# Storing an attention gate's z raw and taking its silu later, in a fused attention and convolution block

## The chip, the cores and the metric

The kernel runs on one core of a Trainium2 chip. A core has TensorE (PE in the profile, with its weight loads as PEld), VectorE (DVE), ScalarE (ACT), GpSimd (POOL) and SyncE (SP); DMAs are issued from the queues of SP, ACT and POOL. The metric is the device time of one execution in microseconds. Before the change the median of three runs is 644.86 us (642.94 to 645.86).

## The reference

One layer of a diffusion transformer on 1024 latent tokens (a grid of 16 rows and 64 columns) of width 1024, with 256 context tokens, all in fp32. The steps that matter here:

```python
h = rmsnorm(x, norm_g) * (1 + scale[:, None]) + shift[:, None]
q, k, v, za, u, bg, cg, zc = jnp.split(h @ w_in, SPLIT_POINTS, axis=-1)   # 8 parts of 512 columns
# q, k: RMS norm per head, rotary; kc, vc: the same columns of the context
attn = neighbourhood_attention(q, k, heads(v), kc, vc, rpb) * jax.nn.silu(za)
conv = bg * centred_short_conv(cg * u, conv_w, conv_b) * jax.nn.silu(zc)
x_new = x + gate[:, None] * (jnp.concatenate([attn, conv], axis=-1) @ w_out)
```

The attention has 8 heads of width 64. A query sees a window of 8 x 16 latent tokens with a learned bias, and all 256 context tokens, in one softmax.

## The kernel before

Every product in fp32 is made of three matmuls on high and low parts (`mm3`, L74 to L76): ACT copies the high part, DVE subtracts to get the low one. The program has three stages.

*Projections.* `h` is made and kept in SBUF with tokens along the free axis. A loop over 4 pairs of heads and 8 token tiles (32 steps, `NT`, and three more to drain) makes q, k and v for a pair, normalises and rotates them and writes them to DRAM (`q_d`, `k_d`, `v_d`). The exponent of that norm is on POOL; ACT does squares, copies and scaling.

*Attention.* It runs as 36 quarters (`quarter(n)`, L1063): quarter n computes scores for the pieces of head n // 4, turns those of quarter n - 2 into probabilities, and multiplies those of quarter n - 3 with v. In a quarter PE first transposes the running maxima `mx` (into `pmx`), DVE takes the row maxima `rm`, PE spreads them back and ACT copies them out as `mg`; DVE subtracts `mg` from the scores `sc` and `sb`, ACT takes exps twice (once rounded, `phc` and `phl`, once full), POOL and DVE subtract to get the low parts `plc` and `pll`. In the same quarter PE makes the new scores `pss` (latent) and `pc` (context, L970; ACT copies them to `sc`), and DVE adds the bias and updates `mx` for the quarter after next. When a head half is done ACT copies its output `po` to `ob` and issues two stores from its own queue, the row sums (`rs_d`) and the output (`o_d`, `finish`, L1035).

*Filler.* The remaining projections, of z for the four pairs (`attn_group(f)`, L484) and of u, c, z and b for three convolution groups (`conv_group`, L384), are units of two halves with four ticks each (`unit(col)`, L338); a tick is six matmuls `pu`. `TICKS` (L33) says how many ticks a quarter takes, so that a unit ends with a quarter: the attention gates' units end with the projections and with quarters 2, 5 and 8, the z units of convolution groups 1 and 2 with quarters 16 and 26, that of group 3 after the quarters. A tick asks for the next unit's weights (`uraw`), ACT and DVE split them (`uh`, `ul`). What a finished unit leaves for ACT and DVE is queued with `chore` and emitted by `do_acts` at the end of a quarter and `do_dves` in the next.

*Gating.* When a pair's last output is stored (quarters 11, 19, 27 and 35), a generator `gated(p)` (L1263) starts, one step a quarter: it loads the row sums, takes reciprocals on DVE, stores them, loads silu(z), the output and the reciprocals of each half, multiplies twice and stores to `y_d`. The last pair is gated in the output stage (`put_y`, L1330).

*Output.* `y` is loaded and split for the eight groups in the order `FORDER`, with `w_out`, and multiplied; six tiles are made group by group, so each group is needed only some 4 us after the one ahead of it.

On PE, ACT, DVE and POOL the program order of the attention is kept as written (the class `ordered`); SP's DMAs may be moved by the scheduler. A queue runs in order. Each DMA has one of eight semaphores, given in turn, and waits until the DMA eight places ahead has landed. ACT loads another function table when the next function is not in the loaded one: silu and exp are in different tables, squares, copies and scaling go with both.

Of the kernel before, what the change touches and what calls it, by code (L numbers as in the profile page):

```python
# [19 lines left out]
P = 128  # L20
# [19 lines left out]
def body(tc, es, x, ctxt, w_ada, b_ada, w_in, q_g, k_g, rpbr, w_out, vecs, cst, out):  # L40
# [49 lines left out]
    def many(name, n, shape):  # L90
        return [dr.tile(shape, F32, name=f"{name}{i}")[:] for i in range(n)]
# [6 lines left out]
    g_d = dr.tile([1, D], F32, name="g_d")  # L98
    rope_d = dr.tile([P, 2048], F32, name="rope_d")
    rs_d = many("rs_d", NPAIR, [2, 2, 512])  # L100
    zs_d = many("zs_d", NPAIR, [P, T])


    q_d = many("q_d", NH, [2, HD, 4, 2, 256])
# [196 lines left out]
    def chore(on_act=None, on_dve=None, queue=soon, frees=None):  # L301
        queue.append([on_act, on_dve, frees])
        if act not in strict:
            do_acts()
            do_dves()

    def do_acts():
        for c in soon + (slow if not any(c[1] and c[1].__name__ == "product" for c in soon) else []):
            if c[0]:
                c[0]()  # L310
                c[0] = None
# [72 lines left out]
    def conv_group(i, done=None):  # L384
# [89 lines left out]
        for part in (gains, gates) if done else (gates, gains):  # L474
            yield from part()

    def silus(z):
        out = []
        for half, ps in z:
            out.append(cvp.tile([P, 512], F32, name="zs", tag="ub", bufs=2))  # L480
            act.activation(out[half], ps, AF.Silu)
        return out

    def attn_group(f):  # L484

        z = []
        for got in unit(z_col(f)):
            if got:
                z.append(got)
            else:  # L490
                yield

        def on_act():
            for half, zs in enumerate(silus(z)):
                sp.dma_start(zs_d[f][:, half * 512:(half + 1) * 512], zs)
        chore(on_act)

    def recip(p, pl):

# [563 lines left out]
    def quarter(n):  # L1063

        live = lambda m: 0 <= m < 4 * NH
        ticks = TICKS[n]
        e, o = n - 2, n - 3  # L1070
        if live(e):
            hd, g = heads[e // 4], e % 4
            pm = psm.tile([P, 512], F32, name="pmx", tag="C", bufs=2)
            for i in range(2):
                pe.transpose(pm[:, i * P:(i + 1) * P], mx[:, (2 * g + i) * P:(2 * g + i + 1) * P], ident)
            rm = ap.tile([P, 2], F32, name="rm", tag="rm", bufs=8)
            dve.tensor_reduce(rm, pm[:, :256].rearrange("p (i k) -> p i k", i=2), AX.X, ALU.max)
        if live(o):
            heads[o // 4].ctx_out(o % 4)
        do_dves(3)  # L1080
        if gating and next(gating[0], "end"):
            gating.clear()
        if live(e):
            for i in range(2):
                pe.transpose(pm[:, 256 + i * P:256 + (i + 1) * P], rm[:, i:i + 1].broadcast_to([P, P]), ident)
            act.copy(mg[:, g * 256:(g + 1) * 256], pm[:, 256:512])
        now = pair_of(n)
        for i, hd_, j in now:
            hd_.scores(j, sbank[:, i])
        if live(n):  # L1090
            heads[n // 4].ctx_scores(n % 4)
        if live(e):
            hd.ctx_exp(g)
        if e in sbs or e in exps:
            pair, sb = pair_of(e), sbs.pop(e)
            w = both(sb, e, pair)
            dve.tensor_tensor(w, w, maxima_of(e, pair), ALU.subtract)
            exps[e] = [ap.tile([P, 2, 384], F32R, name=m, tag=m, bufs=2) for m in ("phl", "pll")]
            ph, pl = (both(v, e, pair) for v in exps[e])
            act.activation(ph, w, AF.Exp)  # L1100
            act.activation(w, w, AF.Exp)
        for _ in range(1):
            next(fill, None)
        done = []
        if o >= 0:
            pho, plo = exps.pop(o)
            for i, hd_, j in pair_of(o):
                hd_.lat_out(j, pho[:, i], plo[:, i])
                if j in (4, 7):
                    done.append((hd_, j // 7))  # L1110
                    if j == 7 and hd_.s:
                        ready.append(hd_.p)
        if now:
            sb = sbs[n] = sb_new()
            g_ = n % 4
            if g_:
                bt = now[0][1].bt
                bias = bt[:, 1:2].broadcast_to([P, 2, 384]) if g_ == 2 else bt[:, 0:2] if g_ == 1 else bt[:, 1:3]
                dve.tensor_tensor(sb, sbank[:, :, :384], bias, ALU.add)
            else:  # L1120
                for i, hd_, j in now:
                    cols = slice(P, 384) if j == 0 else slice(0, 256)
                    dve.tensor_tensor(sb[:, i, :256], sbank[:, i, :256], hd_.bt[:, 1, cols], ALU.add)
            if live(n):
                heads[n // 4].ctx_max(n % 4)
            for i, hd_, j in now:
                hd_.lat_max(j, sb[:, i])
        if e in sbs or e in exps:
            dve.tensor_tensor(pl, w, ph.bitcast(F32), ALU.subtract)
        for _ in range(ticks - 1):  # L1130
            next(fill, None)
        for hd_, bank_ in done:
            hd_.finish(bank_)
        do_acts()
# [32 lines left out]
    for n in range(NT + 3):  # L1167
# [11 lines left out]
            gate.load(n - 1)  # L1179
        if 9 <= n < 25 and n % 2:  # L1180
            next(tables)
        if n == NT - 6:
            heads[0].masks()
            heads[0].load_k()
# [78 lines left out]
    def gated(f):  # L1263

        ri = ap.tile([P, 16], F32, name="ri", tag="ri", bufs=4)
        sp.dma_start(ri, rs_d[f].rearrange("h b (x c) -> (h b x) c", c=16))
        yield
        dve.reciprocal(ri, ri)
        sp.dma_start(ri_d[f].rearrange("h (x c) -> (h x) c", c=16), ri)
        yield  # L1270
        for half in range(2):
            cols = slice(half * 512, (half + 1) * 512)
            zs, tb, rb = (ap.tile([P, 512], F32, name=n, tag=n, bufs=1) for n in ("zs", "tb", "rb"))
            sp.dma_start(zs, zs_d[f][:, cols])
            sp.dma_start(tb, o_d[f][:, cols])
            load_sums(f, half, rb, sp)
            yield
            dve.tensor_tensor(zs, zs, rb, ALU.mult)
            yield
            dve.tensor_tensor(tb, tb, zs, ALU.mult)  # L1280
            sp.dma_start(y_d[f][:, cols], tb)

    with sbuf("att") as ap, psum("psb") as psb:
        sbank = psb.tile([P, 2, 512], F32, name="pss")
        strict[:] = every
        mx = ap.tile([P, T], F32, name="mx")
        sb_new = lambda: ap.tile([P, 2, 384], F32, name="sb", tag="sb", bufs=3)
        mg = ap.tile([P, T], F32, name="mg")
        heads[0].load_v()
        for n in range(4 * NH + 4):  # L1290
            h, g = divmod(n, 4)
            if 0 < h < NH and g == 0:
                heads[h].load_v()
            if h + 1 < NH and g:
                nx = heads[h + 1]
                for load in ((nx.masks, nx.load_q), (nx.load_k,), ())[g - 1]:
                    load()
            quarter(n)
            if ready:
                p = ready.pop()  # L1300
                if p < NPAIR - 1:
                    gating[:] = [gated(p)]
                else:
                    recip(p, ap)
        for _ in fill:
            do_dves()
            do_acts()
        while soon or slow:
            do_dves()
            do_acts()  # L1310
        strict[:] = []
# [18 lines left out]
    def put_y(yp, f):  # L1330

        yh = yp.tile([P, T], F32R, name=f"yh{f}")
        yl = yp.tile([P, T], F32R, name=f"yl{f}")
        for half in range(2):
            cols = slice(half * 512, (half + 1) * 512)
            tb = op.tile([P, 512], F32, name="tb", tag="zt", bufs=4)
            if f == NPAIR - 1:
                zs = op.tile([P, 512], F32, name="zs", tag="zt", bufs=4)
                rb = op.tile([P, 512], F32, name="rb", tag="rb", bufs=2)
                act.dma_start(zs, zs_d[f][:, cols])  # L1340
                act.dma_start(tb, o_d[f][:, cols])
                load_sums(f, half, rb, pool)
                dve.tensor_tensor(zs, zs, rb, ALU.mult)
                dve.tensor_tensor(tb, tb, zs, ALU.mult)
            else:
                act.dma_start(tb, y_d[f][:, cols])
            tv = blocked(tb[:]) if f < NPAIR else by_row(tb[:])
            act.copy(natural(yh[:], half), tv)
            dve.tensor_tensor(natural(yl[:], half), tv, natural(yh[:].bitcast(F32), half), ALU.subtract)
        y[f] = yh, yl  # L1350
# [88 lines left out]
```

## Time and profile before

| | |
|---|---|
| median of three runs | 644.86 us |
| the profiled execution | 644.16 us, span 642.4 us |
| PE busy | 628.7 us (98%) |
| DVE busy | 432.3 us (67%) |
| ACT busy | 322.1 us (50%) |
| POOL busy | 131.6 us (20%) |
| ACT_TABLE_LOAD | 13, 1283 ns each |
| ACT silu of 128x512 | 16, about 600 ns each |

A row of a timeline gives the start in us, the duration, the engine, the line of the kernel, the operation, output<-input by the program's names, the shape, the count of merged instructions and, in brackets, the idle time of the engine just before and what ended it. Most lines read L55, since a recording helper issues the instruction; the names of the tiles tell them apart. `SPq` and `ACTq` are DMA issues. A row of windows gives a stretch, its length and, for each engine, its busy time and its number of instructions. The projections end and quarter 0 begins at about 271.7 us (the first `pss`); the output stage begins at about 550 us.

### The profile page before, as it was taken

What the parts mean: (1) busy time and instruction counts of PE and PEld (TensorE: products, weight loads), DVE (VectorE), ACT (ScalarE), POOL (GpSimd) and SP (SyncE); (2) the same over time, 40 slices, a digit from 0 to 9 for tenths busy, and PEclk for the clock granted to TensorE, in tenths of its full rate; (3) what the DMA queues carried; (4) which work ended last, traced back from release to release, by engine and by line L of the source; (5) the groups of instructions that cost most, each with busy time, mean ns of one, the idle gap of its engine ahead of it and who ended that gap; (6) DMA issues with size and microseconds to landing.
All of it is one profiled execution on the core that took longest, in us unless ns stands there. A gap on an engine that the chain in (4) does not pass through costs nothing.

```text
span 642.4 us, 10301 instructions
## 1 busy us (share of the span) xinstructions
PE 628.7 (98%) x3479; PEld 537.2 (84%) x3480; DVE 432.3 (67%) x819; ACT 322.1 (50%) x692; POOL 131.6 (20%) x138
## 2 busy tenths in 40 slices
PE   8999999999999999999999999999999999999997
PEld 3477898999899999877787888888888888788885
DVE  1677838865766855458787899988998864475111
ACT  3676815524624445347776658565675644352000
POOL 1205005123122222001111121121111111004421
PEclk9999999999999999999999999999999999999999
DMA  8973465868785898799866758785852223875621
GB/s 317 382 255 103 123 221 173 251 210 223 227 276 147 262 273 234 198 233 218 200 161 174 202 146 225 188 212 148 232 144 90 68 89 123 281 239 201 215 100 49
DMA packets 118864, 125.46 MB, mean 195 GB/s; under 512 B 32817, under 2 KB 89353, under 8 KB 117532
## 3 DMA queue, kind: packets, MB, share of 16 engines
q1 hardware_dynamic: 112348, 113.23, 61.0%
q10 hardware_dynamic: 6208, 11.05, 5.6%
q0 software_dynamic: 256, 0.54, 0.3%
q8 instruction: 27, 0.44, 0.3%
q14 instruction: 25, 0.20, 0.1%
HBM read 88.01 MB, written 38.53 MB: 197 GB/s over the span
## 4 chain that ended last, share of the span: by engine, by line
PE 66%; DMA 13%; DVE 9%; SPq 6%; ACT 3%; issue 2%; POOL 1%; ACTq 0%; DVEq 0%; POOLq 0%
PE pu L55 18%; PE pacc L55 18%; DMA k_s<-k_d 5%; PE po L55 5%; PE pout L75 4%; PE pout L76 4%; PE pout L74 4%; SPq L55 3%; PE cacc L55 3%; PE acc L55 2%; PE tr L55 2%; DVE mx L55 2%; DVE sb L55 2%; PE pss L55 2%; PE pmx L55 2%
## 5 line engine op out<-in xcount | busy, mean ns | idle before, releaser
L55 PE MATMUL pu<-h,uh 128*128 128x512 f32 x544 | 169.0, 392 | 0.0
L55 PE MATMUL pacc<-wh,h 128*128 128x384 f32 x512 | 135.3, 338 | 0.0
L55 PEld LDWEIGHTS pu<-h,uh 128*128 128x128 f32 x544 | 98.2, 188 | 17.0
L55 PE MATMUL pu<-h,ul 128*128 128x512 f32 x272 | 106.3, 391 | 0.0
L55 PEld LDWEIGHTS pacc<-wh,h 128*128 128x128 f32 x512 | 92.9, 188 | 0.2 <-ACT qn L55 0.2
L55 POOL TENSOR_TENSOR plc<-sc,phc 128x512 fp32r<-128x512 f32 x32 | 42.6, 1330 | 221.3 <-ACT sc L55 112.3
L55 PE MATMUL pacc<-wl,h 128*128 128x384 f32 x256 | 85.6, 335 | 0.0
L55 POOL TENSOR_TENSOR ss<-ss,few 128x4 f32<-128x4 f32 (+1 forms) x40 | 41.9, 1050 | 127.6 <-DVE ss L55 127.3
L55 PEld LDWEIGHTS pu<-h,ul 128*128 128x128 f32 x272 | 51.1, 188 | 11.2
L55 DVE TENSOR_TENSOR mx<-mx,sb 128x384 f32<-128x384 f32 (+1 forms) x64 | 55.6, 877 | 2.0
L75 PE MATMUL pout<-wol,yh 128*128 128x512 f32 x128 | 49.9, 390 | 0.2 <-DVE wol L1327 0.2
L76 PE MATMUL pout<-woh,yl 128*128 128x512 f32 x128 | 49.6, 389 | 0.0
L74 PE MATMUL pout<-woh,yh 128*128 128x512 f32 x128 | 48.3, 389 | 0.0
L55 PEld LDWEIGHTS pacc<-wl,h 128*128 128x128 f32 x256 | 48.1, 188 | 0.1
L55 DVE TENSOR_REDUCE ss<-sq 128x4 f32<-128x260 f32 (+1 forms) x40 | 15.8, 394 | 46.3 <-ACT sq L55 46.2
L55 ACT COPY mg<-pmx 128x256 f32<-128x256 f32 x32 | 12.0, 374 | 60.1 <-PE pmx L55 48.2
L55 ACT ACTIVATE sq<-pacc 128x256 f32<-128x256 f32 x32 | 12.3, 385 | 53.3 <-PE pacc L55 52.4
L1371 DVE TENSOR_TENSOR ot<-pout,gate 128x512 f32<-128x512 f32 x16 | 10.9, 689 | 37.6 <-PE pout L76 35.3
L55 DVE TENSOR_TENSOR pll<-sb,phl 128x768 fp32r<-128x768 f32 (+2 forms) x33 | 29.3, 889 | 7.5 <-ACT sb L55 7.5
L1372 POOL TENSOR_TENSOR ot<-ot,xr 128x512 f32<-128x512 f32 x15 | 20.1, 1345 | 67.5 <-DVE ot L1371 65.9
L55 ACT ACTIVATE qn<-pacc,ss 128x64 f32<-128x64 f32 x128 | 30.0, 329 | 6.7 <-POOL ss L55 3.2
L55 DVE TENSOR_TENSOR sc<-sc,mg 128x512 f32<-128x512 f32 x32 | 21.9, 683 | 16.4 <-ACT mg L55 16.4
(151 smaller groups left out, 1276.3 us busy)
## 6 DMA issues: line engine op xcount, KB each, us to landing
uraw<-in_w_in SPq DMA_DIRECT2D x34, 256.0 KB
q_d<-qs SPq DMA_DIRECT2D x64, 128.0 KB
k_s<-k_d SPq DMA_DIRECT2D x16, 512.0 KB
q_s<-q_d SPq DMA_DIRECT2D x32, 256.0 KB
wr<-in_w_in SPq DMA_DIRECT2D x40, 192.0 KB
slab<-in_w_ada SPq DMA_DIRECT2D x6, 1024.0 KB
t_d<-btw SPq DMA_DIRECT2D x8, 576.0 KB
bt<-t_d SPq DMA_DIRECT2D x8, 576.0 KB
```

The lines of the kernel that those rows point to most:

```text
L55: i = emit(*a, **kw)
L74: i = pe.matmul(ps, ah, bh, start=first, stop=False)
L75: pe.matmul(ps, ah, bl, start=False, stop=False)
L76: pe.matmul(ps, al, bh, start=False, stop=last)
L1371: dve.tensor_tensor(ot, ps, gate[:, cols], ALU.mult)
L1372: (dve if (nh, t) == (1, NB - 1) else pool).tensor_tensor(ot, ot, xr, ALU.add)
```

## The change

The attention gates' units no longer take the silu when they finish. Each half of z is copied by ACT from PSUM as soon as that half is finished and stored raw in `z_d`. When a pair is gated, both halves of z are loaded at once, at the generator's first step, and put in a list `held`; the next call of `silus`, that of a convolution group's z unit, takes their silu on ACT behind its own, and gating goes on after that. For pair 2 a call of `silus` is queued at once, because no convolution group's unit ends within the quarters after it. For the last pair the silu is taken in the output stage. `gating` becomes a list of generators, worked off one after the other, and what is left of it after the quarters is finished there. An exp of one column in step 29 of the projections has the table of exp loaded there. In quarter 0 the first tick of filler stands ahead of the context scores.

```diff
@@ -98,7 +98,7 @@
     g_d = dr.tile([1, D], F32, name="g_d")
     rope_d = dr.tile([P, 2048], F32, name="rope_d")
     rs_d = many("rs_d", NPAIR, [2, 2, 512])
-    zs_d = many("zs_d", NPAIR, [P, T])
+    z_d = many("z_d", NPAIR, [P, T])
 
 
     q_d = many("q_d", NH, [2, HD, 4, 2, 256])
@@ -474,26 +474,30 @@
         for part in (gains, gates) if done else (gates, gains):
             yield from part()
 
+    held = []
+
     def silus(z):
         out = []
         for half, ps in z:
             out.append(cvp.tile([P, 512], F32, name="zs", tag="ub", bufs=2))
             act.activation(out[half], ps, AF.Silu)
+        while held:
+            for v in held.pop():
+                act.activation(v, v, AF.Silu)
         return out
 
     def attn_group(f):
 
-        z = []
+        def keep(half, ps):
+            z = cvp.tile([P, 512], F32, name="z", tag="ub", bufs=2)
+            act.copy(z, ps)
+            sp.dma_start(z_d[f][:, half * 512:(half + 1) * 512], z)
+
         for got in unit(z_col(f)):
             if got:
-                z.append(got)
+                chore(lambda got=got: keep(*got))
             else:
                 yield
-
-        def on_act():
-            for half, zs in enumerate(silus(z)):
-                sp.dma_start(zs_d[f][:, half * 512:(half + 1) * 512], zs)
-        chore(on_act)
 
     def recip(p, pl):
 
@@ -1079,7 +1083,7 @@
             heads[o // 4].ctx_out(o % 4)
         do_dves(3)
         if gating and next(gating[0], "end"):
-            gating.clear()
+            gating.pop(0)
         if live(e):
             for i in range(2):
                 pe.transpose(pm[:, 256 + i * P:256 + (i + 1) * P], rm[:, i:i + 1].broadcast_to([P, P]), ident)
@@ -1087,6 +1091,9 @@
         now = pair_of(n)
         for i, hd_, j in now:
             hd_.scores(j, sbank[:, i])
+        if n == 0:
+            next(fill)
+            ticks -= 1
         if live(n):
             heads[n // 4].ctx_scores(n % 4)
         if live(e):
@@ -1099,7 +1106,7 @@
             ph, pl = (both(v, e, pair) for v in exps[e])
             act.activation(ph, w, AF.Exp)
             act.activation(w, w, AF.Exp)
-        for _ in range(1):
+        for _ in range(n > 0):
             next(fill, None)
         done = []
         if o >= 0:
@@ -1127,7 +1134,7 @@
                 hd_.lat_max(j, sb[:, i])
         if e in sbs or e in exps:
             dve.tensor_tensor(pl, w, ph.bitcast(F32), ALU.subtract)
-        for _ in range(ticks - 1):
+        for _ in range(ticks - (n > 0)):
             next(fill, None)
         for hd_, bank_ in done:
             hd_.finish(bank_)
@@ -1179,6 +1186,8 @@
             gate.load(n - 1)
         if 9 <= n < 25 and n % 2:
             next(tables)
+        if n == NT - 3:
+            act.activation(few[:, 5:6], ones, AF.Exp)
         if n == NT - 6:
             heads[0].masks()
             heads[0].load_k()
@@ -1264,21 +1273,29 @@
 
         ri = ap.tile([P, 16], F32, name="ri", tag="ri", bufs=4)
         sp.dma_start(ri, rs_d[f].rearrange("h b (x c) -> (h b x) c", c=16))
+        cols = [slice(half * 512, (half + 1) * 512) for half in range(2)]
+        zs = [ap.tile([P, 512], F32, name="zs", tag="zs", bufs=2) for _ in cols]
+        for v, c in zip(zs, cols):
+            sp.dma_start(v, z_d[f][:, c])
         yield
         dve.reciprocal(ri, ri)
         sp.dma_start(ri_d[f].rearrange("h (x c) -> (h x) c", c=16), ri)
+        held.append(zs)
+        if f == NPAIR - 2:
+            chore(lambda: silus(()))
         yield
-        for half in range(2):
-            cols = slice(half * 512, (half + 1) * 512)
-            zs, tb, rb = (ap.tile([P, 512], F32, name=n, tag=n, bufs=1) for n in ("zs", "tb", "rb"))
-            sp.dma_start(zs, zs_d[f][:, cols])
-            sp.dma_start(tb, o_d[f][:, cols])
+        while held:
+            yield
+        for v, c in zip(zs, cols):
+            tb, rb = (ap.tile([P, 512], F32, name=n, tag=n, bufs=1) for n in ("tb", "rb"))
+            half = cols.index(c)
+            sp.dma_start(tb, o_d[f][:, c])
             load_sums(f, half, rb, sp)
             yield
-            dve.tensor_tensor(zs, zs, rb, ALU.mult)
+            dve.tensor_tensor(v, v, rb, ALU.mult)
+            dve.tensor_tensor(tb, tb, v, ALU.mult)
+            sp.dma_start(y_d[f][:, c], tb)
             yield
-            dve.tensor_tensor(tb, tb, zs, ALU.mult)
-            sp.dma_start(y_d[f][:, cols], tb)
 
     with sbuf("att") as ap, psum("psb") as psb:
         sbank = psb.tile([P, 2, 512], F32, name="pss")
@@ -1299,9 +1316,13 @@
             if ready:
                 p = ready.pop()
                 if p < NPAIR - 1:
-                    gating[:] = [gated(p)]
+                    gating.append(gated(p))
                 else:
                     recip(p, ap)
+        for step in gating:
+            for _ in step:
+                do_acts()
+                do_dves()
         for _ in fill:
             do_dves()
             do_acts()
@@ -1337,9 +1358,10 @@
             if f == NPAIR - 1:
                 zs = op.tile([P, 512], F32, name="zs", tag="zt", bufs=4)
                 rb = op.tile([P, 512], F32, name="rb", tag="rb", bufs=2)
-                act.dma_start(zs, zs_d[f][:, cols])
+                act.dma_start(zs, z_d[f][:, cols])
                 act.dma_start(tb, o_d[f][:, cols])
                 load_sums(f, half, rb, pool)
+                act.activation(zs, zs, AF.Silu)
                 dve.tensor_tensor(zs, zs, rb, ALU.mult)
                 dve.tensor_tensor(tb, tb, zs, ALU.mult)
             else:
```

## The prediction

> **What bounds the kernel now.** I read the busy time of each engine first, then the busy time by stage, then by quarter of the attention, and last the timelines of ACT, DVE and PE at the quarters that are too long.
>
> ```profile
> span 642.4 us, 10301 instructions
> ## 1 busy us (share of the span) xinstructions
> PE 628.7 (98%) x3479; PEld 537.2 (84%) x3480; DVE 432.3 (67%) x819; ACT 322.1 (50%) x692; POOL 131.6 (20%) x138
> ```
>
> PE is busy for 628.7 of 642.4 us, so only time in which PE stands or is held up can be won. The profiled execution took 644.16 us, its span and 1.76 us around it; the median of the runs is 644.86 us. I make the sum on this execution and carry it over: predicted median = 644.86 + sum.
>
> ```profile
> core 0: us, PE busy (x) PEld busy (x) DVE busy (x) ACT busy (x) POOL busy (x), PEclk, DMA share, GB/s
> ...
> 262.00:280.00 18.00, 16.95 (x87) 14.27 (x86) 8.32 (x19) 5.89 (x14) 0.00 (x0) 1.00 0.82 221
> 280.00:300.00 20.00, 18.55 (x101) 15.12 (x101) 13.80 (x22) 13.75 (x22) 2.65 (x2) 1.00 0.95 221
> 300.00:320.00 20.00, 19.47 (x113) 15.92 (x111) 16.12 (x25) 14.71 (x23) 4.28 (x3) 1.00 0.92 222
> 320.00:340.00 20.00, 19.54 (x117) 16.38 (x116) 16.99 (x27) 15.48 (x25) 3.35 (x5) 1.00 0.65 164
> 340.00:360.00 20.00, 19.11 (x110) 15.94 (x109) 14.71 (x22) 11.51 (x21) 3.40 (x3) 1.00 0.56 150
> ```
>
> Length less PE busy gives 1.05, 1.45, 0.53, 0.46 and 0.89 us of idle PE: 4.38 us, all in the first 90 us of the attention. Idle time understates it, since PE is also slowed while it waits. So I cut the attention at the first transpose of mx in each quarter. These windows are quarters 3 to 11, then 13 to 17 (the columns as above):
>
> ```profile
> 288.30:295.62 7.32, 7.21 (x41) 5.88 (x39) 5.79 (x9) 7.20 (x12) 1.58 (x2) 1.00 0.91 170
> 295.62:304.16 8.54, 7.72 (x44) 6.15 (x43) 7.35 (x11) 5.36 (x9) 1.74 (x2) 1.00 0.91 252
> 304.16:310.52 6.36, 6.33 (x44) 5.38 (x42) 5.88 (x9) 4.08 (x7) 1.29 (x1) 1.00 1.06 264
> 310.52:318.84 8.32, 7.95 (x42) 6.46 (x43) 5.26 (x9) 6.98 (x11) 1.01 (x1) 1.00 0.87 213
> 318.84:326.79 7.95, 7.62 (x43) 6.23 (x42) 6.80 (x9) 4.96 (x10) 1.98 (x2) 1.00 0.19 49
> 326.79:333.16 6.37, 6.12 (x37) 4.96 (x36) 6.34 (x12) 4.57 (x8) 1.37 (x3) 1.00 0.64 164
> 333.16:340.93 7.77, 7.76 (x48) 6.65 (x49) 5.04 (x9) 6.93 (x11) 1.49 (x1) 1.00 1.08 268
> 340.93:349.46 8.53, 7.85 (x43) 6.29 (x42) 5.14 (x8) 4.42 (x9) 1.30 (x1) 1.00 0.73 197
> 349.46:357.18 7.72, 7.51 (x43) 6.32 (x44) 7.65 (x12) 5.36 (x10) 1.30 (x1) 1.00 0.42 119
> 364.49:372.03 7.54, 7.54 (x50) 6.63 (x48) 7.05 (x11) 4.69 (x8) 1.30 (x1) 1.00 1.05 251
> 372.03:379.58 7.55, 7.55 (x43) 6.43 (x42) 6.47 (x10) 3.27 (x6) 1.29 (x1) 1.00 0.66 168
> 379.58:386.77 7.19, 7.19 (x43) 6.26 (x42) 6.70 (x10) 4.89 (x9) 1.30 (x1) 1.00 0.35 101
> 386.77:394.39 7.62, 7.48 (x43) 6.09 (x42) 7.55 (x14) 5.63 (x10) 1.30 (x1) 1.00 0.66 178
> 394.39:403.53 9.14, 9.14 (x55) 7.79 (x56) 9.04 (x13) 8.29 (x12) 1.29 (x1) 1.00 1.05 276
> ```
>
> ```profile
> 352.51 1.38 PE pu L55 x6
> ```
>
> Quarters repeat with a period of four, and quarters 13 to 16 stand for the four kinds without stalls: 7.54, 7.55, 7.19 and 7.62 us at three ticks. One tick of filler is 1.38 us; quarters 5 and 8 have one tick fewer, quarter 17 one more. Against these the surplus of quarters 3 to 11 is 0.13, 0.92, 0.20, 0.77, 0.76, 0.13, 0.23, 0.98 and 0.53: 4.65 us. Together with the 1.05 us ahead of them, some 5.7 us is the ceiling of what this change can reach there. DVE works 7.05 to 7.55 us in quarters that stall hardly at all, so it is nearly full but keeps up when nothing holds it.
>
> **The change, part by part.** *Table loads.* A silu among exps costs ACT two loads.
>
> ```profile
> L55 ACT ACT_TABLE_LOAD x13 | 16.7, 1283 | 0.9 <-PEq L1422 0.7
> ```
> ```profile
> 288.88 1.28 ACT L55 ACT_TABLE_LOAD   x1
> 290.18 1.09 ACT L55 ACTIVATE zs<-pu 128x512 f32<-128x512 f32 x2
> 291.15 0.38 ACT L55 COPY mg<-pmx 128x256 f32<-128x256 f32 x1
> 291.40 0.62 ACT L55 COPY sc<-pc 128x512 f32<-128x512 f32 x1
> 292.04 1.28 ACT L55 ACT_TABLE_LOAD   x1
> ```
> ```profile
> 291.56 0.69 DVE L55 TENSOR_TENSOR sc<-sc,mg 128x512 f32<-128x512 f32 x1 [1.38 <-ACT mg L55]
> ```
> ```profile
> 296.54 0.33 PE L55 MATMUL pmx<-ci,mx 128*128 128x128 f32 x1 [0.65 <-DVE mx L55]
> ```
>
> Before, seven of the thirteen loads lie in quarters 2 to 9: one ahead of the first exp, three pairs around the attention gates' silus. The changed program has none there: nine loads in all, one moved into the projections, two new ones in quarter 33. That frees 7 x 1.28 = 9.0 us of ACT. The copies of z take the place of silus of the same shape (0.62 against 1.09 / 2), so nothing is won or lost by them. Only what reaches PE counts. The rows show the path: the load and the silus hold the copy of mg, DVE waits 1.38 us for mg, its maximum mx comes late, PE stands 0.65 us at the head of quarter 4. With the copy some 1.1 us earlier mx is in time: I take 0.8 of quarter 4's 0.92, and the 0.1 of quarter 3. In quarters 6 and 7 (1.53 us) the second load holds the exps and so POOL's plc and DVE's pll, but mg waits there for other things too, and DVE is back to back ahead of quarter 6: I take 0.6 (bounds 0 and 1.5). Of quarters 5, 8 and 9 (0.56), where the tick count is low and DVE full, 0.2 (bounds 0 and 0.56).
>
> The Trainium skill, page "ScalarE: Activation LUTs", section "What ACT_TABLE_LOAD costs", puts a switch at about 1283 ns for the load and 1380 ns for a drain. The load agrees (1283 ns); of a drain beside it these rows show nothing, the silu starting 1.30 us after the load does. By the page's price seven loads would free 18.6 us of ACT instead of 9.0; the ceiling on PE stays the same.
>
> *The load in the projections* (1.28 us, and an exp of one column): ACT there waits for PE's projection tile, so both are hidden; without that cover they would cost 1.3 us once.
>
> ```profile
> 254.88 0.38 ACT L55 ACTIVATE sq<-pacc 128x256 f32<-128x256 f32 x1 [2.79 <-PE pacc L55]
> ```
>
> *The first tick of quarter 0* goes ahead of the context scores. PE stood there for a PSUM buffer that DVE's qs frees; the tick (1.38 us) covers the wait whole:
>
> ```profile
> 273.28 0.74 PE L55 MATMUL pc<-q_s,kc_s 128*128 128x256 f32 x4 [1.05 <-DVE qs L55]
> ```
>
> I take 1.05 (bounds 0, if the wait comes back at the next quarter's scores, and 1.05).
>
> *DMAs.* SP issues the same eight stores and eight loads of z as before; POOL's queue is untouched. The stores go out a half at a time, four ticks earlier for the first half, and gating's loads both at once instead of a half each. But each DMA waits, in the program, for the one eight places ahead on a shared semaphore, so changed places change what ACT's two stores of ob wait for, and ACT's copy of mg stands behind them:
>
> ```profile
> 344.42 0.45 ACTq L1040 DMA_DIRECT2D o_d<-ob  x1
> 344.97 0.37 ACT L55 COPY mg<-pmx 128x256 f32<-128x256 f32 x1 [3.71 <-DMA rs_d<-ob]
> ```
> ```profile
> 349.46 0.30 PE L55 MATMUL pmx<-ci,mx 128*128 128x128 f32 x1 [0.52 <-DVE mx L55]
> ```
>
> Here the store waited for the second half of a k_s load, and this makes most of the 1.51 us of quarters 10 and 11. In the changed program the later of the two stores waits for the first half. I take 0.8 (bounds -1.5, if another quarter is held so, and 1.5).
>
> *Silus held back.* Two more silus (1.09 us) run after the convolution's own in quarters 16 and 26, ahead of mg, sc and the exps of the next quarter. Their z is asked for at least three quarters earlier (for pair 2 only once quarter 30 has freed the buffer), so they should not wait. ACT is busy 8.29 of 9.14 us in quarter 17 and becomes full; PE uses these exps a quarter later, and DVE has gating's products of these quarters moved off it. I take a loss of 0.1 each (bounds 0 and 1.1 each). For pair 2 a load, two silus and a load stand in quarter 33 (3.65 us) ahead of one split of weights, which PE needs in the next quarter; I take 0.1 (bounds 0 and the whole 3.65).
>
> *Gating of pair 2* ends after the quarters, pair 3's silus stand in the output stage. The products fall into DVE's wait for the last row sums, the silus into ACT's wait for output weights; I take 0. Without the cover they cost 1.4 and 1.1 us.
>
> ```profile
> 539.53 0.25 DVE L55 RECIPROCAL ri<-ri 128x16 f32<-128x16 f32 x1 [6.29 <-DMA ri<-rs_d]
> ```
> ```profile
> 569.92 0.62 ACT L1326 CAST woh<-woraw 128x512 fp32r<-128x512 f32 x1 [2.72 <-DMA woraw<-in_w_out]
> ```
>
> Sum: -(0.8 + 0.1 + 0.6 + 0.2 + 1.05 + 0.8) + 0.2 + 0.1 = -3.25 us, so 644.86 - 3.25 = 641.6 us; the profiled execution would become 640.9.
>
> **The rivals.** *B, the loads were not the limit.* Once ACT is early, mx waits for DVE, which is nearly full, or for the same DMA landings. For it: quarters 5 and 8, where DVE works 5.88 us in 6.36 and 6.34 in 6.37; against it: quarters 13 to 16, as full and without stalls. Then quarter 0 and half of quarter 4 remain: -1.05 - 0.45, 643.4 us.
>
> *C, every stall goes.* Quarters 13 to 16 show that the code can run so. Then -5.7, 639.2 us. Against it: DVE runs back to back ahead of quarter 6, and nothing in the change lightens that.
>
> *D, slower: ACT is held at the head of its queue by a DMA* in more quarters than now, because places on the shared semaphores moved and the z loads add two 256 KB pieces to the bursts of loads. One hold like that at 344.97 is worth up to 1.51 us (quarters 10 and 11). Three more eat the gain; five, with all else but B's 1.5 lost, give 644.86 + 7.5 - 1.5 = 650.9 us. For it: DMA shares of 0.91 to 1.08 in four of the nine early quarters. Against it: quarters 13 to 17 have the same stores, and PE shows no such stall. The Trainium skill, page "PSUM — Partial Sum Buffer", section "Engine vs sequencer instructions", says that ScalarE's queue is strictly first in, first out; the row at 344.97 agrees, a copy that needs no DMA standing behind a store for 3.71 us.
>
> That no load leaves the quarters is excluded by the changed program's own order of instructions.
>
> **How the numbers follow.** My forecast (639.9 to 642.9) 0.52; B (642.9 to 645) 0.24; C (below 639.9) 0.13; D (above 645) 0.11. A measurement of this kernel tells about 0.5%, 3.2 us, from no change. Faster, below 641.6: 1.7 of the forecast's 3.0 us (0.29) and all of C, 0.42; slower, above 648.1: most of D, 0.08; the rest, 0.50, within. The range takes in C's value and the near part of D: 639.0 to 646.0.
>
> **What would show it.** Right: nine table loads, none between quarter 2 and 15; the 1.05 us ahead of pc gone; quarter 4 at 7.6 to 7.8 us; the mg wait behind o_d in quarter 10 near 1.5 us; quarters 17 and 27 no more than 0.2 longer. Wrong: quarters 4, 6, 7 and 10 as long as now with DVE waiting for nothing (B); an ACT idle ahead of mg put down to a DMA in quarters that had none (D); a wait for z ahead of the silus of quarters 16, 26 or 33; PE standing in the output stage.

## The result, and the profile after

The changed kernel takes 649.76 us (median of 7 runs, 647.02 to 653.66) against 644.31 us (7 runs, 642.85 to 645.86): a ratio of 1.0091, 95% interval 1.0068 to 1.0114. It is 5 to 6 us slower, where I had forecast 3 us faster. Its profiled execution took 653.66 us with a span of 651.9; it is the longest of the seven, so the profile shows a loss of 9.5 us where the medians show 5.45.

The page of the kernel after, and from its groups of instructions the table loads:

```profile
span 651.9 us, 10304 instructions
...
PE 632.8 (97%) x3480; PEld 541.0 (83%) x3480; DVE 436.5 (67%) x819; ACT 321.3 (49%) x697; POOL 130.2 (20%) x138
```
```profile
L55 ACT ACT_TABLE_LOAD x9 | 11.5, 1283 | 2.6 <-DVE sb L55 1.7 <-PEq L1444 0.7
```

The change did what it says: nine loads instead of thirteen. Yet PE's busy time grew by 4.1 us with the same matmuls, and its idle time by 5.4 us. To find where, I cut both traces at the same instructions: the first transpose of mx in quarters 2, 6, 8, 22, 24 and 33, the first matmul of pout, and the end. Windows of the kernel before (us from the span's start; then busy us of each engine with the number of its instructions, the granted clock of PE, the share of the DMA engines, GB/s):

```profile
0.00:281.86 281.86, 276.46 (x1604) 242.36 (x1606) 178.22 (x433) 136.66 (x389) 65.31 (x79) 1.00 0.75 228
281.86:310.52 28.66, 27.18 (x155) 22.34 (x153) 23.38 (x36) 20.82 (x33) 5.24 (x4) 1.00 0.98 231
310.52:326.79 16.27, 15.57 (x84) 12.70 (x85) 12.06 (x18) 11.93 (x20) 2.99 (x2) 1.00 0.54 133
326.79:434.60 107.81, 106.52 (x619) 90.25 (x618) 94.94 (x145) 70.31 (x116) 18.49 (x18) 1.00 0.76 193
434.60:449.35 14.75, 14.75 (x86) 12.69 (x84) 12.41 (x20) 8.58 (x15) 2.60 (x2) 1.00 0.54 146
449.35:519.96 70.61, 70.47 (x404) 59.80 (x402) 61.81 (x95) 43.97 (x72) 12.17 (x11) 1.00 0.48 133
519.96:550.21 30.25, 30.25 (x152) 25.25 (x151) 17.31 (x28) 14.30 (x23) 4.68 (x7) 1.00 0.38 117
550.21:642.40 92.19, 87.52 (x385) 71.81 (x383) 32.12 (x48) 15.58 (x26) 20.07 (x15) 0.99 0.52 179
```

and of the kernel after:

```profile
0.00:281.52 281.52, 277.40 (x1605) 242.43 (x1606) 178.12 (x433) 138.18 (x392) 64.54 (x79) 1.00 0.75 227
281.52:308.80 27.28, 26.65 (x155) 22.46 (x153) 24.03 (x36) 17.64 (x32) 5.23 (x4) 1.00 0.99 225
308.80:332.07 23.27, 18.10 (x84) 15.06 (x85) 11.83 (x18) 9.32 (x18) 2.75 (x2) 0.85 0.55 137
332.07:437.88 105.81, 105.55 (x619) 90.46 (x618) 95.88 (x143) 68.17 (x115) 18.41 (x18) 1.00 0.75 189
437.88:454.42 16.54, 15.26 (x86) 12.65 (x85) 12.20 (x20) 8.49 (x15) 2.59 (x2) 1.00 0.62 159
454.42:524.27 69.85, 69.85 (x404) 59.88 (x402) 62.36 (x93) 44.85 (x74) 11.91 (x11) 1.00 0.45 121
524.27:555.67 31.40, 30.69 (x152) 25.00 (x150) 16.08 (x27) 16.12 (x25) 4.70 (x7) 1.00 0.43 133
555.67:651.90 96.23, 89.25 (x384) 73.08 (x384) 35.98 (x53) 18.53 (x31) 20.05 (x15) 0.98 0.51 176
```

Read the lengths against each other. Four stretches are shorter: up to quarter 2 by 0.34 us, quarters 2 to 5 by 1.38, quarters 8 to 21 by 2.00, quarters 24 to 32 by 0.76, together 4.5 us. Four are longer: quarters 6 and 7 by 7.00, quarters 22 and 23 by 1.79, the stretch from quarter 33 to the output stage by 1.15 and the output stage by 4.04, together 14.0 us. In the two that lost most the granted clock is below 1.00 (0.85 and 0.98; before, 1.00 and 0.99).

The single quarters that I had named, after (3, 4, 6, 7, 10 and 11):

```profile
287.96:294.83 6.87, 6.87 (x40) 5.92 (x39) 6.11 (x10) 4.29 (x7) 1.30 (x1) 1.00 0.94 174
294.83:302.41 7.58, 7.50 (x44) 6.20 (x42) 6.39 (x10) 4.70 (x8) 1.29 (x1) 1.00 0.88 242
...
308.80:322.02 13.22, 8.11 (x42) 6.36 (x43) 5.55 (x9) 3.87 (x8) 1.27 (x1) 0.96 0.87 211
322.02:332.07 10.05, 9.99 (x42) 8.70 (x43) 6.27 (x10) 5.45 (x10) 1.48 (x1) 0.71 0.14 39
346.22:353.74 7.52, 7.52 (x43) 6.41 (x42) 5.84 (x9) 4.79 (x9) 1.30 (x1) 1.00 0.72 188
353.74:360.95 7.21, 7.21 (x43) 6.27 (x42) 6.72 (x10) 4.67 (x8) 1.29 (x1) 1.00 0.45 130
```

Quarters 3, 4, 10 and 11 lost 0.45, 0.96, 1.01 and 0.51 us: the gain is there. Quarter 6 took 4.90 us more and quarter 7 2.10 more.

**Quarter 6.** ACT's timeline after, and the first matmul that PE could do again:

```profile
308.33 0.56 ACT L55 COPY ob<-po 65x512 f32<-65x512 f32 x1
308.81 0.59 ACT L55 COPY z<-pu 128x512 f32<-128x512 f32 x1
316.43 0.50 ACTq L1043 DMA_DIRECT2D rs_d<-ob  x1
316.97 0.50 ACTq L1044 DMA_DIRECT2D o_d<-ob  x1
317.57 0.37 ACT L55 COPY mg<-pmx 128x256 f32<-128x256 f32 x1 [8.18 <-PE pu L55]
```
```profile
322.02 0.97 PE L55 MATMUL pmx<-ci,mx 128*128 128x128 f32 x2 [4.75 <-DVE mx L55]
```

and ACT at the same place in the kernel before:

```profile
310.05 0.56 ACT L55 COPY ob<-po 65x512 f32<-65x512 f32 x1
310.63 1.28 ACT L55 ACT_TABLE_LOAD   x1
310.91 0.49 ACTq L1039 DMA_DIRECT2D rs_d<-ob  x1
311.92 1.08 ACT L55 ACTIVATE zs<-pu 128x512 f32<-128x512 f32 x2
313.63 0.51 ACTq L1040 DMA_DIRECT2D o_d<-ob  x1
314.23 0.37 ACT L55 COPY mg<-pmx 128x256 f32<-128x256 f32 x1 [1.22 <-PE pc L55]
```

After, the two stores of ob are issued 8 us after the copy that they store, and mg stands behind them for 8.18 us although the transposes that it copies had ended at 310.93. The releaser printed beside it (PE pu) is not the one: the issue of the store ends just before mg. Each store waits, by the program's shared semaphores, for a DMA eight places ahead, and those are loads of k_s and v for the next head, in a burst at a DMA share of 0.99. The two halves of k_s, after and then before, as SP asks for them:

```profile
303.03 1.10 SPq L949 DMA_DIRECT2D k_s<-k_d  x2
```
```profile
302.10 1.10 SPq L945 DMA_DIRECT2D k_s<-k_d  x2
```

The traces hold each DMA's semaphore and the time at which it landed. After, the store of row sums waits for the second half of k_s, which landed at 316.35, 0.08 us ahead of the issue at 316.43; the first half had landed at 314.54. Before, it waited for the first half, landed at 310.83, and the store of the output for a load of v, landed at 313.60. So the store's place is now one transfer later, 1.8 us by these landings, and the transfers themselves land later. Before, the same wait was there, but a table load and two silus lay in it, so that ACT stood for 1.22 us only; and of gating's z loads one (issued at 293.88) was in that burst, where two are now (295.76). In quarter 22 the store waits for a z load itself (issued at 429.96, landed at 441.25).

### The profile page after: what moved, and what is told of

It reads as the page before. It is cut to its first block, busy times and chain, and to the rows that moved or that the text cites. A ratio compares the mean times of both kernels' runs of the same rounds, so it can differ in the third digit from the quotient of the medians.

```text
span 651.9 us, 10304 instructions
## 1 busy us (share of the span) xinstructions
PE 632.8 (97%) x3480; PEld 541.0 (83%) x3480; DVE 436.5 (67%) x819; ACT 321.3 (49%) x697; POOL 130.2 (20%) x138
## 4 chain that ended last, share of the span: by engine, by line
PE 70%; DMA 12%; DVE 6%; SPq 4%; ACT 3%; issue 2%; POOL 1%; ACTq 0%; DVEq 0%; POOLq 0%
PE pu L55 18%; PE pacc L55 17%; PE po L55 5%; PE pout L74 4%; PE pout L75 4%; PE pout L76 4%; PE tr L55 3%; PE acc L55 3%; SPq L55 3%; PE cacc L55 3%; PE pss L55 2%; DMA uraw<-in_w_in 2%; DMA k_s<-k_d 2%; PE pmx L55 2%; DMA zs<-z_d 2%
## 5 line engine op out<-in xcount | busy, mean ns | idle before, releaser
L55 DVE TENSOR_TENSOR mx<-mx,sb 128x384 f32<-128x384 f32 (+1 forms) x64 | 58.7, 925 | 2.0
```

The costliest lines, as they stand in the source:

```text
L55: i = emit(*a, **kw)
```

## The experiments

The theories: 1, ACT's queue is held by the stores of ob; 2, the rest is lost in the output stage, behind pair 2's gating; 3, the bytes in the burst set how long the hold is. The rivals stand in the expectations. Times are medians; ratios are to the kernel before on the same chip, with their 95% intervals.

**The changed kernel again**, unaltered.

> The changed kernel once more, unaltered, for a second profile. Theory 1 (the order of the DMAs decides: ACT's store of row sums in quarter 6 waits for the second half of the k_s load, which is 1 us later and has 256 KB more ahead of it than before): the hold of ACT in quarter 6 comes again, 5 us or more where the first profile had 8.18, PE stands 3 us or more there, and the time is 647 to 653 us. Rival (one unlucky execution of a transfer): no hold over 3 us in quarter 6, holds in other places, or none and the time lies well under 647.

650.50 us, ratio 1.0090 (1.0061 to 1.0120). The hold came again at the same place, 8.35 us, with PE standing 4.89; so did the waits for woh, 4.0 us in all. It is no accident of one execution.

**The stores of ob on SP.**

```diff
-            act.dma_start(rs_d[self.p][self.s, bank:bank + 1], ob[64:65])
-            act.dma_start(o_d[self.p][...], ob[0:64])
+            sp.dma_start(rs_d[self.p][self.s, bank:bank + 1], ob[64:65])
+            sp.dma_start(o_d[self.p][...], ob[0:64])
```

> The changed kernel with the two stores of ob issued by SP instead of ACT. Theory 1 (ACT's queue is held behind these stores, 8.18 us in quarter 6 and 4.89 us in quarter 22, and PE pays 4.75 and 1.08 us and a lowered clock for it): both holds go, quarters 6 and 7 together fall from 23.3 us to about 16, quarter 22 and 23 from 16.5 to about 15, the output stage stays as it is: about 9 us less in the profile, 642 to 645 us. Rival (the load of k_s itself is late, whoever waits for it): the hold moves to PE's scores or to SP's loads, and the time stays at 647 or more.

645.24 us, ratio 1.0014 (0.9993 to 1.0034). Quarters 6 and 7 took 8.35 and 7.19 us, 22 and 23 7.55 and 7.19: the holds are gone, as theory 1 says, and quarter 33 began at 513.93 instead of 519.96 in the kernel before. A new wait took back most of it: SP issued the last row sums late, DVE's RECIPROCAL waited for them, and the split of weights behind it let PE stand for 4.16 us:

```profile
539.99 0.25 DVE L55 RECIPROCAL ri<-ri 128x16 f32<-128x16 f32 x1 [8.82 <-DMA ri<-rs_d]
```

**Gating's loads of z held back.**

```diff
         for v, c in zip(zs, cols):
+            pool.memset(v[:, 0:1], 0.0)
             sp.dma_start(v, z_d[f][:, c])
```

> The changed kernel with gating's two loads of z held back to the quarter that asks for them (each tile gets a one-column memset on POOL first), so that they leave the burst of loads in quarter 4. Theory 1: the k_s load lands 1 to 2 us earlier and the store of quarter 6 waits for its first half again, as in the kernel before: quarters 6 and 7 fall from 23.3 to about 16 us, the output stage stays: 643 to 646 us. Rival (the hold comes from the stores of raw z or from PE asking earlier, not from gating's loads): quarter 6 keeps a hold of 5 us or more, 647 or more.

646.67 us, ratio 1.0039 (1.0021 to 1.0058), a little above what I expected. The hold in quarter 6 fell to 4.72 us, PE's stand to 1.30, quarters 6 and 7 to 9.78 and 7.73, not to 16: earlier loads shorten the hold and do not remove it. The second half of k_s landed 31.4 us after the head of quarter 2 (34.8 in the changed kernel), and the store still waited for that half, not for the first as I had expected. The output stage kept its waits for woh (3.6 us), and quarter 22 its hold (4.36 us; the quarter took 8.26).

**Two parts of the change alone**, in the kernel before.

```diff
+        if n == 0:
+            next(fill)
+            ticks -= 1
         if live(n):
             heads[n // 4].ctx_scores(n % 4)
...
-        for _ in range(1):
+        for _ in range(n > 0):
             next(fill, None)
...
+        if n == NT - 3:
+            act.activation(few[:, 5:6], ones, AF.Exp)
```

> The kernel before with two parts of the change alone: the first tick of quarter 0 ahead of the context scores, and the load of the exp table in the projections; silu stays at the gate units. The order of the DMAs stays that of the kernel before. Theory 1: these parts are harmless and worth little, 0 to 1.2 us less than the kernel before (643.1 to 644.4 us), quarter 0 without its wait of 1.05 us. Rival (the earlier tick or the early exp table is what shifts the attention against its loads and brings the hold): slower than before, 646 us or more.

644.02 us, ratio 0.9994 (0.9979 to 1.0009). The wait of 1.05 us is gone: from the last projection matmul to quarter 2 it takes 21.21 us instead of 22.50. But quarters 6 and 7 took 8.57 and 8.80 instead of 8.33 and 7.95, 1.09 more: an earlier start alone meets the same loads. The exp table loaded early saves nothing in this run: the silu at the end of the projections throws it out again, so that there are 15 table loads where the kernel before has 13.

**Pair 2's gating in the output stage**, with the stores on ACT.

```diff
+        if f == NPAIR - 2:
+            yield
+            dve.reciprocal(ri, ri)
+            sp.dma_start(ri_d[f].rearrange("h (x c) -> (h x) c", c=16), ri)
+            return
...
-        if f == NPAIR - 2:
-            chore(lambda: silus(()))
...
-            if f == NPAIR - 1:
+            if NPAIR - 2 <= f < NPAIR:
                 zs = op.tile([P, 512], F32, name="zs", tag="zt", bufs=4)
```

> The changed kernel with pair 2's silu and its two products moved into the output stage, as pair 3 has them; its row sums are inverted in quarter 33 as before. Theory 2 (what PE waits for in the output stage, 3.0 and 4.0 us for woh, comes from pair 2's gating that is drained after the quarters: its second half is stored at 551.3 and ACT's loads of y and the casts of woh stand behind that): PE waits under 0.5 us for woh, the output stage begins some 30.3 us after the head of quarter 33 as in the kernel before instead of 31.4 to 31.9, quarters 6 and 7 stay at 23 us: 4 to 5 us less than the changed kernel, 645 to 647. Rival (the loads of the output stage are late by themselves, because the quarters ended late): the waits for woh stay at 2 us or more, 649 to 651.

647.02 us, ratio 1.0039 (1.0013 to 1.0065). PE waits for woh no more; the output stage begins 30.30 us after quarter 33, and from its first to its last matmul it takes 86.90 us, against 91.33 in the changed kernel and 87.28 in the kernel before. Quarters 6 and 7 were 20.2 us instead of the 23 expected, with a hold of 5.97 us. The program up to there is that of the changed kernel, whose two profiles had 8.18 and 8.35 us; why this hold was 2 us shorter is not settled.

What stood in PE's way there, in the changed kernel (SP's queue, then ACT with its queue, then PE):

```profile
545.04 0.35 SPq L1292 DMA_DIRECT2D tb<-o_d  x1
551.31 0.32 SPq L1297 DMA_DIRECT2D y_d<-tb  x1
```
```profile
550.53 0.34 ACTq L1344 DMA_DIRECT2D woraw<-in_w_out  x1
554.12 0.33 ACTq L1368 DMA_DIRECT2D tb<-y_d  x1
554.48 0.62 ACT L1370 CAST yh<-tb 128x512 fp32r<-128x512 f32 x1 [6.97 <-DMA y_d<-tb]
...
557.11 0.42 ACTq L1344 DMA_DIRECT2D woraw<-in_w_out  x1
562.19 0.33 ACTq L1368 DMA_DIRECT2D tb<-y_d  x1
562.55 0.62 ACT L1347 CAST woh<-woraw 128x512 fp32r<-128x512 f32 x1 [5.06 <-DMA tb<-y_d]
```
```profile
563.22 3.22 PE L74 MATMUL pout<-woh,yh 128*128 128x512 f32 x7 [2.47 <-ACT woh L1347]
```

Pair 2's second half is asked for at 545.04, when its one buffer is free, and stored at 551.31. The first groups of the output stage do not need it: pair 2 is the sixth in `FORDER`. What holds ACT is again the shared semaphores, by the times in the trace. Its load of weights at 550.53 has the semaphore of the load asked for at 545.04, which landed at 550.51. Its load of y at 554.12, of a convolution group stored at 496, has that of pair 2's store, which landed at 554.04. Its load of y at 562.19 has that of the load at 554.12, which landed at 562.11. The cast at 562.55, for which PE waits, stands behind this last load in ACT's queue; the weights that it copies had landed at 553.34.

**The stores of ob on POOL**, first in the changed kernel, then with pair 2's gating in the output stage as well, then in the kernel before.

```diff
-            act.dma_start(rs_d[self.p][self.s, bank:bank + 1], ob[64:65])
-            act.dma_start(o_d[self.p][...], ob[0:64])
+            pool.dma_start(rs_d[self.p][self.s, bank:bank + 1], ob[64:65])
+            pool.dma_start(o_d[self.p][...], ob[0:64])
```

> The changed kernel with the two stores of ob issued by POOL, whose DMAs have semaphores of their own, instead of ACT. Theory 1: no hold of ACT in quarters 6 and 22, quarters 6 and 7 at 15.5 to 16 us, 22 and 23 at 14.8; SP is not burdened as it was when SP issued them, so the wait of 4.2 us for the weights' split before the output stage is not there; the waits for woh stay at 3 to 4 us: 642 to 645 us. Rival (POOL is late with plc when it issues the stores): PE waits for plc, 646 or more.

643.37 us, ratio 0.9978 (0.9961 to 0.9996). No hold: quarters 6 and 7 took 8.33 and 7.19 us, 22 and 23 7.56 and 7.19. The waits for woh stay, 4.4 us.

> Both together: the stores of ob on POOL, pair 2's gating in the output stage. If theories 1 and 2 hold and add, all that the changed kernel lost comes back and what its table loads free stays: quarter 33 begins 5 to 6 us earlier than in the kernel before, the output stage 30.3 us later: 638 to 641 us. Rival (the two losses cover one another, or the output stage's loads cannot come earlier): 642 or more.

638.45 us, ratio 0.9891 (0.9870 to 0.9911). Quarter 33 begins at 514.93, the output stage 30.23 us later. The two losses do not cover one another: POOL's stores alone are worth 6.4 us to the changed kernel, pair 2 alone 2.7, both together 11.3, more than the sum (differences of medians from different rounds, in which the kernel before took 644.31 and 644.50).

> The kernel before with the stores of ob on POOL, all else unchanged: what the stores cost there, without raw z. Theory 1: quarters 10 and 11 lose their 1.5 us of stalls, quarters 4, 6 and 7 keep theirs since the table loads make them: 642 to 643.5 us. The difference to the run with raw z, POOL's stores and pair 2 in the output stage is then what raw z is worth by itself: 2 to 4 us. Rival (the table loads are no limit once the stores are off ACT): quarters 4, 6 and 7 come down as well, 640 to 642, and raw z is worth nothing.

642.93 us, ratio 0.9971 (0.9956 to 0.9985). Quarters 10 and 11 lost 1.14 us, quarter 4 stayed at 8.52; quarter 7 fell from 7.95 to 7.23, which I had put down to the table loads. What is left in quarter 10, 7.90 us, is taken up below.

**Fewer bytes in the burst.** Gating's loads of z carry 16 of 512 columns; silu and products are taken of these alone, so most of that gating is left out.

```diff
-            sp.dma_start(v, z_d[f][:, c])
+            sp.dma_start(v[:, 0:16], z_d[f][:, c][:, 0:16])
```

> The changed kernel with gating's loads of z cut to 16 of 512 columns each (silu and product are taken of those 16 columns alone, so most of the gating of pairs 0 to 2 is left out). Every DMA keeps its place in the order and its semaphore; what goes is 0.5 MB of the burst ahead of the k_s and v loads of quarter 5. Theory 3 (the burst is at its limit, so its bytes set when the v load lands on which the store of ob waits): at the 215 to 298 GB/s of these stretches 0.5 MB are 1.8 to 2.4 us; the hold in quarter 6 goes from 8.2 to some 6 us, PE stands 2.3 to 2.9 instead of 4.8: 645 to 648 us. Rival (the places on the semaphores alone decide): the hold stays at 8 us and quarters 6 and 7 at 23, 648 or more.

The hold in quarter 6, and PE behind it:

```profile
316.57 0.37 ACT L55 COPY mg<-pmx 128x256 f32<-128x256 f32 x1 [6.18 <-DMA rs_d<-ob]
```
```profile
321.02 0.30 PE L55 MATMUL pmx<-ci,mx 128*128 128x128 f32 x1 [2.71 <-DVE mx L55]
```

Some 6 and 2.3 to 2.9 us were expected; it is 6.18 and 2.71, with the stores waiting for the same transfers as in the changed kernel. That agrees with theory 3 but does not show it: this is one profile, and 5.97 us came in the run with pair 2 in the output stage with all bytes in place. Counted from the head of quarter 2, the second half of k_s landed after 32.8 us here, and in the eight profiles with two full z loads in the burst after 32.7 to 35.5 us. Only with z held back (31.4 us) does it fall outside that range, and there order and bytes changed together. So it is likely, not shown, that the z loads lengthen the hold; how much of it is bytes, place or chance stays open. Quarters 22 and 23 were not lengthened (7.54 and 7.26 us); quarters 14 and 15 were, by 0.7 us together, with a hold of 3.77 us. The time, 644.02 us, ratio 0.9995 (0.9976 to 1.0014), is below my 645 to 648, since pair 2's chain was shorter too and PE did not wait for woh.

**What raw z is worth.** Silu back at the gate units, in the kernel with POOL's stores and pair 2's products in the output stage:

```diff
-            act.copy(z, ps)
-            sp.dma_start(z_d[f][:, half * 512:(half + 1) * 512], z)
+            for half, zs in enumerate(silus(z)):
+                sp.dma_start(z_d[f][:, half * 512:(half + 1) * 512], zs)
...
-                act.activation(zs, zs, AF.Silu)
```

> The kernel with POOL's stores and pair 2's products in the output stage, but silu taken at the attention's gate units as in the kernel before (its stored value is loaded where raw z was); everything else stays, the first tick of quarter 0 and the early exp table too. The difference to the run with raw z is what raw z is worth when nothing else stands in its way. My prediction's terms for the table loads (quarters 3, 4, 6, 7, 5, 8 and 9: 1.7 us) and the 3.1 us by which quarter 33 came earlier after quarter 2 between POOL's stores with and without raw z give 1.7 to 3.1 us: 640.2 to 641.6. Rival (the loads of k_s and v set the early quarters once ACT's hold is gone): within 0.5 of the run with raw z, below 639.

> The changed kernel with POOL's stores and pair 2's products in the output stage, unaltered, beside the run with silu at the gate units: 638 to 639 us.

641.09 us with silu at the gate units (ratio 0.9958, 0.9944 to 0.9973), 638.10 us with raw z (0.9911, 0.9892 to 0.9931): 3.0 us. The run with silu at the gate units has 15 table loads against 7, two more than the kernel before, for the reason given above. Not all of the 3.0 us is table loads. Of the quarters, 3 and 4 give 0.42 and 0.96 of it, and 10 gives 0.35: a table load in quarter 9 makes the exps late, and DVE's pll waits 1.18 us for them. Quarters 5 to 9 give 0.06 together. Quarters 16 and 24 give 0.31 and 0.81, but no load went there: gating does not wait for a silu in that run, so DVE's products fall into quarters 15, 17, 23 and 25, where with raw z they stand in 18, 20, 28 and 30. In quarter 24 it is even 0.63 us slower than the kernel before (8.13 against 7.50), so the 3.0 us is somewhat too much for raw z alone.

The page and PE's waits from quarter 2 on, of the kernel with raw z, POOL's stores and pair 2 in the output stage, which is faster than both kernels of this case:

```profile
span 635.5 us, 10311 instructions
...
PE 626.2 (99%) x3479; PEld 537.7 (85%) x3480; DVE 436.9 (69%) x819; ACT 318.4 (50%) x695; POOL 150.0 (24%) x174
```
```profile
PE pmx L55 <- DVE rm L55: 0.7, 2, 0.5
PE pmx L55 <- DVE mx L55: 0.5, 2, 0.3
```

## Why the prediction was wrong

- *Table loads* (-1.7 us in all): right in sum, by luck; the places were half wrong. In quarters 3 and 4 the mechanism held: they lost 0.45 and 0.96 us where I took 0.1 and 0.8. In quarters 5 to 9 I took 0.8, and the last pair of runs shows 0.06 there; quarter 7's surplus went when the stores of ob did (POOL). Quarter 10 has 0.35 us of table loads that I had put under the DMAs. B, that the loads were not the limit, is refuted for quarters 3 and 4 and borne out for 5 to 9.
- *First tick of quarter 0* (-1.05): the stall went; from the last projection matmul to quarter 2 it takes 1.27 us less, and 1.29 in the run with this part alone. Alone it is worth nothing that the times show, since quarters 6 and 7 gave back 1.09 us. That was the bound of 0 which I named, only later than I looked for it.
- *DMAs* (-0.8, between -1.5 and 1.5): this term failed, and with it the forecast. Quarters 10 and 11 gained 1.52 us, the whole upper bound, though some 0.35 of it belongs to the table loads. But the step that bounded the other side by "one hold like that at 344.97" was wrong: I took the price of every hold from the one that I saw. The hold that came cost 7.00 us in quarters 6 and 7, and another 1.79 in 22 and 23. What I should have read is in the timeline of the kernel before: the store at 313.63 was waiting already, with a table load and two silus inside the wait. The change takes that work out, starts earlier, moves the store one transfer back (1.8 us) and puts a second z load into the same burst; the runs do not part these shares. Rival D had the mechanism right but asked for five holds of 1.5 us; one long one and a short one in the quarters, and ACT's loads in the output stage, were enough. That its 650.9 us lies near the 649.76 measured is luck.
- *Held silus* (+0.2): right or better. Quarters 16 and 17 and quarters 26 and 27 became 0.51 and 0.39 us shorter; DVE had less to do there (15.54 us busy instead of 16.59 in 16 and 17). Quarter 16, which I had counted among those without stalls, fell from 7.62 to 7.32 us.
- *Quarter 33* (+0.1): right; to the next quarter's first product with v it takes 7.72 us before and 7.71 after.
- *Exp table in the projections* (0): not resolved. From the first to the last projection matmul it takes 181.26 us before and 181.65 and 180.85 in the two profiles after.
- *Gating of pair 2 after the quarters* (0): this term failed too, by 5.2 us (1.15 up to the output stage and 4.04 in it). The cover I named was there for DVE: RECIPROCAL still waited 4.78 us. But I followed only the engines that do the work, and not the semaphores: pair 2's load and store, now at the end, share them with ACT's loads for the output stage, and a cast that PE waits for stands behind those. The sign "PE standing in the output stage" came.
- *The clock* was in no term: every row that I had read showed 1.00.

## What to carry to other kernels

When a change removes work from an engine's queue, look for a DMA issue in the same queue that waits behind or beside that work: the work may have been hiding the wait. Price a hold not by the smallest one in the trace but by when the transfer that it waits for lands, and add that the clock can fall if PE stands (here from 2.47 us on). A store that other queues can issue belongs on the engine with nothing urgent behind it, and work that is moved past the end of a loop has to be followed through its loads and stores, to whoever waits on the same semaphores.

## What I had not expected of the hardware

PE's granted clock fell to one half at stands of 2.47 us and more, for some 3 to 6 us. Windows of the changed kernel, from the stand in quarter 6 on (the clock is the third number from the end):

```profile
317.27:322.02 4.75, 0.01 (x1) 0.03 (x1) 3.90 (x6) 3.27 (x6) 1.27 (x1) 0.90 0.58 155
322.02:324.02 2.00, 1.94 (x8) 1.65 (x9) 1.44 (x3) 0.00 (x0) 0.00 (x0) 0.50 0.00 0
...
328.02:330.02 2.00, 2.00 (x13) 1.68 (x12) 1.11 (x2) 1.94 (x4) 1.18 (x1) 1.00 0.40 131
```

In the profiles of this case, from quarter 0 on, single stands of 2.47, 2.53, 2.55, 2.71, 3.29, 4.16, 4.75 and 4.89 us were each followed by a clock of 0.50 to 0.55 in the lowest 2 us after them; one of 2.34 and all of 1.43 or less were not. It adds to the price of a stand: quarter 7 took 10.05 us after the stand and 7.19 where the stores were on SP, 2.86 us on top of 4.75. The Trainium skill, page "TensorE: Matmul & The Clock Gate", section "Part 1: The HAM clock gate", says that an idle window of about 3.4 us halves the clock and that the window runs freely; the half clock agrees, but here 2.47 us were enough. By the rule that the Trainium skill gives in the same part, no idle gaps of PE over about 3.4 us, five of these eight stands would have been harmless. With only one stand between 1.43 and 2.47 us, no run here shows where a limit lies, or that it is a fixed one.

An issue of a store costs ACT or SP 0.2 to 0.5 us of its queue; on POOL the two took 0.54 and 0.55 us of the engine on average, and no wait of PE came of it.
